# Differential attention with q and k projected feature-major, rotary rows exchanged by DMA, and attention steps split into probabilities and values

## The chip, the cores and the metric

One core of one Trainium2 chip runs the whole program. The metric is the time of one execution in microseconds, as the device measures it; the profiled execution has a span (first to last instruction) beside its time. PE is the matrix engine, DVE the vector engine, ACT the scalar engine, POOL the general engine, SP the engine that issues most of the DMA transfers. The weight loads of PE are shown as PEld; they run beside its matmuls.

## What is computed

Two layers work on 512 tokens x and 256 context tokens, 1024 wide. Each layer normalises, projects with `w_in`, and mixes three ways: differential attention (DA, 4 heads), grouped-query attention (GQ, 8 heads) and a long convolution (hyena); the three are gated and projected with `w_out`. The second layer needs its context tokens only as keys and values. The part that the change touches is DA:

```python
def _rope_1d(x, cos, sin):
    x1, x2 = jnp.split(x.astype(jnp.float32), 2, axis=-1)
    return jnp.concatenate([x1 * cos - x2 * sin, x2 * cos + x1 * sin], axis=-1)
...
def _diff_attend(q, k, v, lam):
    scale = DA_QK_DIM ** -0.5
    def body(qb):
        s = jnp.einsum('bqhcd,bkhcd->bhcqk', qb, k).astype(jnp.float32) * scale
        p = jax.nn.softmax(s, axis=-1)
        a = (p[:, :, 0] - lam * p[:, :, 1]).astype(v.dtype)
        return jnp.einsum('bhqk,bkhe->bqhe', a, v)
...
    ka_all = jnp.concatenate([ka_c, _rope_2d(ka, tab_da)], axis=1)
    oa = _rms(_diff_attend(qa, ka, va, lam), da_subln_g) * (1.0 - lam_init)
```

A head has two maps (c = 0 and 1) with 64 features each for q and k, and 128 features for v. Queries and keys of x are rotated, those of the context are not.

## The kernel before

Every fp32 product is made of three matmuls on split operands (high and low part, `mm3`, L138 to L140): high by high, high by low, low by high. There are two shapes of projection. `proj_tok` gives a pair of token tiles, tokens on partitions and features along the row: 48 matmuls of 128x256 (pst<-wh,hT). `proj_feat` gives 128 features on partitions and all tokens along the row: 24 matmuls of 128x512 for x or of 128x256 for the context (psf<-hT,wh). The token pairs are numbered 0 and 1 (x) and 2 (context).

In time a layer runs: hyena, GQ (its attention from about 280 to 560 us in layer 0, 1120 to 1360 in layer 1), DA (560 to 765 and 1330 to 1475) and `w_out` (px<-wh,yT).

DA works head by head. For each pair of x the kernel projects q and k together with `proj_tok`, rotates them in the token-major layout (DVE L1039 by the cosine, two DVE L1043 by the sine, two POOL L1046 that combine the halves), and turns the result with four PE transposes (L1050) into the same PSUM bank, features on partitions. `evac_q` copies a pair with its scale (ACT L1012) and leaves high and low parts of the two maps on opposite halves of the partitions (DVE L1015); `evac_k` makes a high tile and a low tile (ACT L1024, DVE L1027, L1028, ACT L1029, POOL memset L1023). The context's q and k come feature-major from `proj_feat` and go through the same two functions.

Attention runs in the background of the projections. A step of `da_att` is one query pair of one head: for each half of 128 queries and each map, scores S (PE L628, L629: one pair of matmuls per key pair), maximum (DVE L634), exponential (ACT L637), reciprocal; then the weighted difference of the two maps (ACT L965, DVE L966); and in the same step `pv`: transposes T of the probabilities P (PE L648), their split into ph (ACT L581) and pl (DVE L582), and the value matmuls O (PE L655 and L656 with ph, L658 with pl), followed by norm and gate. `gq_att` has the same form with a query pair of one head per step. A generator yields after each step; `att.spread(steps, units)` spreads the steps over the projections that follow, and each projection advances them. From the program's order a list scheduler with a model of the engines' times then sets the order of each engine's queue, and interleaves freely; each engine executes its own queue strictly in that order.

The buffers that set limits are: score banks S two, T one, O one, projection banks two; six P tiles, five ph/pl tiles, five tiles in the pool of the rotary temporaries, twenty tiles for q, k and v. SP issues nearly all loads and stores in order (weights raw<-in_w_in, gates gl<-gd, results yx<-tah and yx<-y, reloads yld<-yx); POOL issues the tables and yT loads.

## Time and profile before

| | us |
|---|---|
| median of 3 runs | 1595.95 (1593.34 to 1599.08) |
| profiled execution, its own time | 1593.43 |
| its span | 1591.7 |
| granted clock, mean | 0.989 |

The profile of that one execution gives, for each engine, its busy time; for windows of time the same with the granted clock of PE; and for an instruction that waits the one that released it. Matmuls overlap, so the time that one costs is read from the distance between two starts, not from its duration. The rows that matter stand below.

### The profile page before, as it was taken

What the parts mean: (1) busy time and instruction counts of PE and PEld (TensorE: products, weight loads), DVE (VectorE), ACT (ScalarE), POOL (GpSimd) and SP (SyncE); (2) the same over time, 40 slices, a digit from 0 to 9 for tenths busy, and PEclk for the clock granted to TensorE, in tenths of its full rate; (3) what the DMA queues carried; (4) which work ended last, traced back from release to release, by engine and by line L of the source; (5) the groups of instructions that cost most, each with busy time, mean ns of one, the idle gap of its engine ahead of it and who ended that gap; (6) DMA issues with size and microseconds to landing.
All of it is one profiled execution on the core that took longest, in us unless ns stands there. A gap on an engine that the chain in (4) does not pass through costs nothing.

```text
span 1591.7 us, 29098 instructions
## 1 busy us (share of the span) xinstructions
PE 1510.1 (95%) x11126; PEld 1398.6 (88%) x11126; DVE 1127.6 (71%) x2222; ACT 830.9 (52%) x1673; POOL 415.6 (26%) x451
## 2 busy tenths in 40 slices
PE   5989999999999999998999999999999999898997
PEld 3768889999898989798999977888999998898997
DVE  6789667877776475777755378869877756768755
ACT  5645243555556555566653256334546556656643
POOL 0243443212212141113002114334222222214032
PEclk9999999999999999999999999999999999999999
DMA  9437676423435253315352334674422232115441
GB/s 344 145 111 263 192 222 200 129 76 96 143 102 169 93 159 117 113 48 195 117 179 94 93 108 145 213 229 146 152 75 87 87 97 87 57 51 182 130 133 70
DMA packets 105952, 216.87 MB, mean 136 GB/s; under 512 B 11345, under 2 KB 54291, under 8 KB 105812
## 3 DMA queue, kind: packets, MB, share of 16 engines
q1 hardware_dynamic: 95300, 178.56, 34.9%
q0 software_dynamic: 9936, 35.39, 7.3%
q8 instruction: 88, 1.44, 0.4%
q10 hardware_dynamic: 576, 1.05, 0.2%
q14 instruction: 52, 0.43, 0.1%
HBM read 174.45 MB, written 40.52 MB: 135 GB/s over the span
## 4 chain that ended last, share of the span: by engine, by line
PE 79%; DVE 9%; DMA 4%; issue 3%; ACT 3%; POOL 1%; SPq 0%; POOLq 0%; DVEq 0%; ACTq 0%
PE psf L138 7%; PE psf L139 7%; PE psf L140 7%; PE pst L138 6%; PE pst L140 6%; PE pst L139 6%; PE px L138 4%; PE px L140 4%; PE px L139 4%; PE T L648 4%; PE O L658 2%; PE O L655 2%; PE O L656 2%; PE S L138 2%; PE S L140 2%
## 5 line engine op out<-in xcount | busy, mean ns | idle before, releaser
L138 PE MATMUL psf<-hT,wh 128*128 128x512 f32 (+1 forms) x768 | 267.9, 353 | 8.8 <-DVE cv L687 5.0
L138 PE MATMUL pst<-wh,hT 128*128 128x256 f32 x960 | 273.8, 285 | 0.2
L139 PE MATMUL pst<-wl,hT 128*128 128x256 f32 x960 | 273.7, 285 | 0.0
L140 PE MATMUL pst<-wh,hT 128*128 128x256 f32 x960 | 273.6, 285 | 0.0
L139 PE MATMUL psf<-hT,wh 128*128 128x512 f32 (+1 forms) x768 | 268.4, 350 | 0.0
L140 PE MATMUL psf<-hT,wl 128*128 128x512 f32 (+1 forms) x768 | 268.2, 349 | 0.0
L156 DVE TENSOR_TENSOR wl<-raw,wh 128x1024 fp32r<-128x1024 f32 x136 | 174.6, 1285 | 40.1 <-ACT wh L152 38.7
L152 ACT ACTIVATE wh<-raw 128x1024 fp32r<-128x1024 f32 x136 | 143.5, 1056 | 90.1 <-PE psf L139 34.7
L140 PEld LDWEIGHTS pst<-wh,hT 128*128 128x128 f32 x960 | 183.9, 192 | 1.7 <-issue 1.7
L138 PEld LDWEIGHTS pst<-wh,hT 128*128 128x128 f32 x960 | 184.0, 192 | 1.6 <-issue 1.1
L139 PEld LDWEIGHTS pst<-wl,hT 128*128 128x128 f32 x960 | 183.9, 192 | 0.2
L138 PE MATMUL px<-wh,yT 128*128 128x256 f32 x640 | 181.6, 284 | 1.1 <-DMA yT<-yx 0.6
L140 PE MATMUL px<-wh,yT 128*128 128x256 f32 x640 | 181.6, 284 | 0.2 <-DVE yT L1083 0.2
L139 PE MATMUL px<-wl,yT 128*128 128x256 f32 x640 | 181.5, 284 | 0.0
L637 ACT ACTIVATE P<-S,sa 128x768 f32<-128x768 f32 (+1 forms) x160 | 130.2, 814 | 87.3 <-DVE sa L634 59.1
L138 PEld LDWEIGHTS psf<-hT,wh 128*128 128x128 f32 x768 | 146.3, 191 | 29.0 <-ACT kH L1029 3.2
L140 PEld LDWEIGHTS psf<-hT,wl 128*128 128x128 f32 x768 | 146.5, 191 | 17.9 <-issue 0.8
L139 PEld LDWEIGHTS psf<-hT,wh 128*128 128x128 f32 x768 | 146.9, 191 | 17.3 <-issue 1.2
L634 DVE TENSOR_REDUCE sa<-S 128x1 f32<-128x768 f32 (+1 forms) x160 | 134.6, 841 | 21.8 <-PE S L140 11.9
L582 DVE TENSOR_TENSOR pl<-T,ph 128x512 fp32r<-128x512 f32 x156 | 107.1, 687 | 49.0 <-ACT ph L581 44.2
L581 ACT ACTIVATE ph<-T 128x512 fp32r<-128x512 f32 x156 | 92.7, 594 | 86.5 <-PE T L648 85.6
L138 PEld LDWEIGHTS px<-wh,yT 128*128 128x128 f32 x640 | 122.1, 191 | 2.1 <-ACT pm L1152 0.9
(300 smaller groups left out, 3559.8 us busy)
## 6 DMA issues: line engine op xcount, KB each, us to landing
raw<-in_w_in SPq DMA_DIRECT2D x104, 512.0 KB, 4.1
adaw<-in_ada_w SPq DMA_DIRECT2D x32, 512.0 KB, 4.4
raw<-in_w_out SPq DMA_DIRECT2D x32, 512.0 KB, 3.8
tab<-in_inv POOLq DMA_DIRECT2D x20, 512.0 KB, 4.6
tab<-in_fwd POOLq DMA_DIRECT2D x18, 512.0 KB, 5.1
adaw<-in_ada SPq DMA_DIRECT2D x16, 512.0 KB, 10.7
yT<-yx POOLq DMA_DIRECT2D x16, 512.0 KB, 7.1
gl<-gd SPq DMA_DIRECT2D x60, 128.0 KB, 2.3
```

The lines of the kernel that those rows point to most:

```text
L138: i0 = PE.matmul(ps, sh, mh, start=first, stop=False)
L139: PE.matmul(ps, sh, ml, start=False, stop=False)
L140: return i0, PE.matmul(ps, sl, mh, start=False, stop=last)
L152: ACT.activation(hi, src, AF.Copy)
L156: last_lo[0] = e.tensor_tensor(out=lo, in0=src, in1=hi.bitcast(F32), op=ALU.subtract)
L581: ACT.activation(dh, ps, AF.Copy)
L582: return DVE.tensor_tensor(out=dl, in0=ps, in1=dh.bitcast(F32), op=ALU.subtract)
L634: DVE.tensor_reduce(out=nm, in_=S[:, :n], axis=AX.X, op=ALU.max, negate=True)
L637: ACT.activation(P[:, :n], S[:, :n], AF.Exp, bias=nm, accum_out=s)
L648: PE.transpose(T[:, kk, q * 128:(q + 1) * 128], aa[q][:, (2 * i + kk) * 128:(2 * i + kk + 1) * 128], ident)
L655: PE.matmul(O, vh, ph[:, kk], start=(i == 0 and kk == 0), stop=False)
L656: PE.matmul(O, vl, ph[:, kk], start=False, stop=False)
```

## The change

First, q and k of x in DA are projected feature-major. `rope_feat(qk)` runs `proj_feat` for q (0) or k (1): ACT copies the bank to v (dv), SP issues four transfers of 32x512 (64 KB each) from v to w (dw) that swap neighbouring groups of 32 rows, DVE multiplies the bank by the cosines (L1061, df), POOL multiplies w by the sines (L1062), DVE adds the two (L1063). The tables cosD and sinD are laid out to suit, 128x512 each instead of 128x128. `evac_q` then reads halves of the sum, and `evac_k` reads all 512 columns at once into a high and a low tile per map (ACT, DVE L1049 and L1050, POOL L1047).

Second, the scores of an x query have one pair of matmuls for the 512 x keys and one pair for the 256 context keys.

Third, attention steps are skewed: `skewed` runs the probabilities of step n and then the values of step n - 1, with one more step at the end, in GQ and in DA; the gate's load moves into the values.

Fourth, the program is built with a descriptor scratch of 8192 for DMAs that software generates.

```diff
         def scores_c(c, q, kT, klist, i):
             S = pS.tile([128, 1024], F32, tag="S", name="S")
             m = slice(i * 128, (i + 1) * 128)
-            for n, kp in enumerate(klist):
-                kh, kl = kT[kp]
-                ps = S[:, n * 256:(n + 1) * 256]
-                PE.matmul(ps, q[:, c, m], kh[:, c], start=True, stop=False)
-                PE.matmul(ps, q[:, c, m], kl[:, c], start=False, stop=True)
+            for isx, lo in ([(True, 0), (False, 512)] if len(klist) > 1 else [(False, 0)]):
+                kh, kl = kT[isx]
+                ps = S[:, lo:lo + (L if isx else LC)]
+                PE.matmul(ps, q[:, c, m], kh[c], start=True, stop=False)
+                PE.matmul(ps, q[:, c, m], kl[c], start=False, stop=True)
             return S
...
+        def skewed(steps, probs, values):
+            ahead = None
+            for step in steps:
+                if step[0] != 1:
+                    slow.tick()
+                aa = probs(*step)
+                if ahead:
+                    values(*ahead)
+                ahead = (*step, aa)
+                yield
+            values(*ahead)
+            yield
...
+            yield from skewed([(j, hh) for j in qpairs for hh in range(2)], probs, values)
...
-                att.spread(2 * len(qpairs), nq + {(0, 0): -full, (0, 1): 3, (1, 0): 0, (1, 1): 1}[g, c])
+                att.spread(2 * len(qpairs) + 1, nq + {(0, 0): -full, (0, 1): 3, (1, 0): 0, (1, 1): 1}[g, c])
...
+            yield from skewed([(j,) for j in qpairs], probs, values)
...
-                def evac_k(p, ps):
-                    kh = up.tile([128, 2, 256], F32R, tag="u", name="kH")
-                    kl = up.tile([128, 2, 256], F32R, tag="u", name="kL")
+                def evac_k(isx, src):
+                    n = L if isx else LC
+                    if isx:
+                        kh, kl = [[up.tile([128, n], F32R, tag="u", name=nm) for _ in range(2)] for nm in ("kH", "kL")]
+                    else:
+                        kh, kl = [up.tile([128, 2, n], F32R, tag="u", name=nm) for nm in ("kH", "kL")]
+                        kh, kl = [[v[:, c] for c in range(2)] for v in (kh, kl)]
                     for c in range(2):
-                        POOL.memset(kl[64 - 64 * c:128 - 64 * c, c].bitcast(F32), 0.0)
...
+                        r, o = slice(64 * c, 64 * c + 64), slice(64 - 64 * c, 128 - 64 * c)
+                        POOL.memset(kl[c][o].bitcast(F32), 0.0)
+                        ACT.activation(kh[c][r], src[r], AF.Copy)
+                        DVE.tensor_tensor(out=kl[c][r], in0=src[r], in1=kh[c][r].bitcast(F32), op=ALU.subtract)
+                        DVE.tensor_copy(kh[c][o], kh[c][r].bitcast(F32))
+                    kT[isx] = (kh, kl)
...
-                for p in (0, 1):
-                    ps = proj_tok(W, p)
...
-                    DVE.tensor_tensor(out=t1.rearrange("p t c (h d) -> p t (c h) d", d=32),
-                                      in0=ps.rearrange("p t (c d) -> p t c d", d=32), in1=cb, op=ALU.mult)
...
-                    for qk in range(2):
-                        for t in range(2):
-                            PE.transpose(ps[:, qk, t * 128:(t + 1) * 128],
-                                         t1[:, t, 2 * qk:2 * qk + 2].rearrange("p c d -> p (c d)"), ident)
-                    evac_q(p, ps[:, 0])
-                    evac_k(p, ps[:, 1])
+                def rope_feat(qk):
+                    ps = proj_feat(W, qk, True)
+                    v = tp.tile([128, L], F32, tag="tp", name="dv")
+                    ACT.activation(v, ps, AF.Copy)
+                    w = tp.tile([128, L], F32, tag="tp", name="dw")
+                    for i in range(4):
+                        SP.dma_start(w[32 * i:32 * i + 32], v[32 * (i ^ 1):32 * (i ^ 1) + 32])
+                    f = tp.tile([128, L], F32, tag="tp", name="df")
+                    DVE.tensor_tensor(out=f, in0=ps, in1=cosD, op=ALU.mult)
+                    POOL.tensor_tensor(out=w, in0=w, in1=sinD, op=ALU.mult)
+                    DVE.tensor_tensor(out=f, in0=f, in1=w, op=ALU.add)
+                    return f
+
+                f = rope_feat(0)
+                for p in range(2):
+                    evac_q(p, f[:, p * 256:(p + 1) * 256])
+                evac_k(True, rope_feat(1))
                 if full:
                     evac_q(2, proj_feat(W, 0, False))
-                evac_k(2, proj_feat(W, 1, False))
+                evac_k(False, proj_feat(W, 1, False))
                 att.add(da_att(head, hh, V, qT, kT))
-                att.spread(len(qpairs), {0: nq, 1: 3 + nq - ng, 2: nq - ng, 3: 1}[head])
+                att.spread(len(qpairs) + 1, {0: nq, 1: 3 + nq - ng, 2: nq - ng, 3: 1}[head])
...
-    cosD = cp.tile([128, 4, 32], F32, tag="cosD", name="cosD")
+    cosD = cp.tile([128, L], F32, tag="cosD", name="cosD")
...
-    nc = _bacc.Bacc("TRN2", target_bir_lowering=False, num_devices=1)
+    nc = _bacc.Bacc("TRN2", target_bir_lowering=False, num_devices=1, dynamic_dma_scratch_size=8192)
```

How the queues of the engines change is shown at two places. On PE in the last DA steps of layer 1, between matmuls of `w_out`, the queue before reads, with S the scores, T the transposed probabilities, and O the values:

```order
L628 MATMUL S<-kH,qT 128x256
L629 MATMUL S<-kL,qT 128x256
L648 MATMUL T<-ident,P 128x128 x3
L655 MATMUL O<-ph,vh 128x256
L656 MATMUL O<-ph,vl 128x256
L655 MATMUL O<-ph,vh 128x256
L656 MATMUL O<-ph,vl 128x256
L658 MATMUL O<-pl,vh 128x256 x2
L648 MATMUL T<-ident,P 128x128
L628 MATMUL S<-kH,qT 128x256
```

and the queue of the changed kernel, at the place that answers to it:

```order
L628 MATMUL S<-kH,qT 128x512
L629 MATMUL S<-kL,qT 128x512
L628 MATMUL S<-kH,qT 128x256
L629 MATMUL S<-kL,qT 128x256
L648 MATMUL T<-ident,P 128x128 x4
L655 MATMUL O<-ph,vh 128x256
L656 MATMUL O<-ph,vl 128x256
L655 MATMUL O<-ph,vh 128x256
L656 MATMUL O<-ph,vl 128x256
L658 MATMUL O<-pl,vh 128x256 x2
L655 MATMUL O<-ph,vh 128x256
```

The scores of the next step now stand ahead of T, with 512 columns and 256; all four T of a key pair are followed at once by their O, and a second run of O follows directly.

On DVE at the rotary of the second DA head of layer 0 the queue before reads, with pst the projection's bank and t_8236 to t_8310 the rotary's temporaries:

```order
L1039 TENSOR_TENSOR t_8236<-pst,cosD 128x512
L1043 TENSOR_TENSOR t_8237<-pst,sinD 128x8x32 x2
L582 TENSOR_TENSOR pl<-T,ph 128x512
L1015 SCALAR_TENSOR_TENSOR qT<-pst,qT 64x256 x2
L1027 TENSOR_TENSOR kL<-pst,kH 64x256 x2
L1028 CAST kH<-kH 64x256
L1039 TENSOR_TENSOR t_8309<-pst,cosD 128x512
L1043 TENSOR_TENSOR t_8310<-pst,sinD 128x8x32 x2
```

and in the changed kernel, at the same head, with psf the bank, df the product with the cosines and dw the exchanged rows:

```order
L1061 TENSOR_TENSOR df<-psf,cosD 128x512
L582 TENSOR_TENSOR pl<-T,ph 128x512
L1063 TENSOR_TENSOR df<-df,dw 128x512
L1034 SCALAR_TENSOR_TENSOR qT<-df,qT 64x256 x4
L639 RECIPROCAL sa<-sa 128x1
L634 TENSOR_REDUCE sa<-S 128x1
L582 TENSOR_TENSOR pl<-T,ph 128x512
L1061 TENSOR_TENSOR df<-psf,cosD 128x512
L639 RECIPROCAL sa<-sa 128x1
L891 TENSOR_SCALAR P<-P,sa 128x256
L634 TENSOR_REDUCE sa<-S 128x1
L910 SCALAR_TENSOR_TENSOR y<-O,cols_250,gl 128x256
```

The multiplication L1061 and the sum L1063 of a rotary, which needs the exchanged rows, have one other operation between them for q; for k the sum comes two rows below this piece. Before, the combination was POOL's and DVE went on. On SP the eight exchanges of that head stand as one block between the stores and loads of gates and results and the loads of weights:

```order
L578 DMA gd_174<-sg 128x512
L578 DMA gd_174<-sg 128x256
L1059 DMA dw<-dv 32x512 x8
L915 DMA yx_6_125<-tah 128x256
L669 DMA gl<-gd_170 128x256
L915 DMA yx_6_125<-tal 128x256
L396 DMA adaw<-in_ada_w 128x1024 x2
L528 DMA raw<-in_w_in 128x1024 x2
```

Before, no transfer belonged to the rotary, and the rows around the block followed each other directly.

## Rows read from the trace of the kernel before

**Rows 1.** The page: busy time of each engine, share of the span, instructions.

```profile
PE 1510.1 (95%) x11126; PEld 1398.6 (88%) x11126; DVE 1127.6 (71%) x2222; ACT 830.9 (52%) x1673; POOL 415.6 (26%) x451
```

**Rows 2.** Windows: us, then busy PE, PEld, DVE, ACT, POOL; PEclk, DMA share, GB/s.

```profile
280.00:560.00 280.00, 280.00 (x2124) 260.57 (x2124) 199.64 (x438) 156.37 (x338) 59.89 (x62) 1.00 0.37 116
...
720.00:765.00 45.00, 40.36 (x306) 38.80 (x304) 34.90 (x70) 29.76 (x58) 14.38 (x25) 0.92 0.60 194
...
1370.00:1400.00 30.00, 26.50 (x201) 25.24 (x202) 20.13 (x43) 16.58 (x34) 5.29 (x9) 0.94 0.18 58
...
sum 270.00, PE 248.04 PEld 233.96 DVE 202.46 ACT 172.04 POOL 66.21; mean PE 35.43 PEld 33.42 DVE 28.92 ACT 24.58 POOL 9.46
```

**Rows 3.** Waits of PE, whole span: engine, line, releaser: us, times, longest.

```profile
PE O L655 <- ACT ph L581: 6.2, 6, 3.0
...
PE O L658 <- DVE pl L582: 3.3, 7, 1.2
...
PE S L628 <- ACT P L637: 2.9, 6, 0.6
...
PE pst L1050 <- POOL t L1046: 1.5, 1, 1.5
```

**Rows 4.** Timeline of PE, layer 0, DA's first head: start us, us, line, operation.

```profile
565.80 0.28 PE L140 MATMUL pst<-wh,hT 128*128 128x256 f32 x1
...
567.12 0.60 PE L1050 MATMUL pst<-ident,t 128*128 128x128 f32 x4
...
567.67 0.28 PE L140 MATMUL pst<-wh,hT 128*128 128x256 f32 x1
```

**Rows 5.** Timeline of PE in a stretch of feature-major projection.

```profile
229.84 0.39 PE L138 MATMUL psf<-hT,wh 128*128 128x512 f32 x1
...
231.43 0.39 PE L139 MATMUL psf<-hT,wh 128*128 128x512 f32 x1
```

**Rows 6.** Lines by form: busy, mean ns of one | idle before.

```profile
L1039 DVE TENSOR_TENSOR t<-pst,cosD 128x512 f32<-128x512 f32 x16 | 11.0, 686 | 7.4 <-PE pst L140 7.4
...
L1043 DVE TENSOR_TENSOR t<-pst,sinD 128x256 f32<-128x256 f32 x32 | 12.0, 415 | 0.0
...
L1046 POOL TENSOR_TENSOR t<-t,t 128x256 f32<-128x256 f32 x32 | 24.2, 776 | 55.0 <-DVE t L1043 41.2 <-issue 11.9 <-DVE sa L639 1.8
...
L574 ACT ACTIVATE gv<-psf 128x512 f32<-128x512 f32 x24 | 14.2, 593 | 20.5 <-PE psf L140 16.6 <-issue 3.8
...
L604 POOL TENSOR_TENSOR t<-t,t 128x512 f32<-128x512 f32 x16 | 21.6, 1350 | 59.9 <-DVE t L602 44.6 <-PE S L140 6.5 <-DVE sm L171 5.9
...
L577 DVE TENSOR_TENSOR sg<-gv,sg 128x512 f32<-128x512 f32 x24 | 17.5, 731 | 2.8 <-ACT sg L183 2.8
```

**Rows 7.** DMA issues: KB each, median us from issue to landing.

```profile
yx<-tah SPq DMA_DIRECT2D x32, 128.0 KB, 1.8
```

**Rows 8.** Timeline of SP's queue in a DA stretch.

```profile
644.75 0.38 SPq L669 DMA_DIRECT2D gl<-gd  x1
```

**Rows 9.** Timeline of PE: T groups with O directly behind them.

```profile
1370.82 0.60 PE L648 MATMUL T<-ident,P 128*128 128x128 f32 x4
...
1372.10 0.38 PE L655 MATMUL O<-ph,vv 128*128 128x256 f32 x1 [0.69 <-ACT ph L581]
...
1439.71 0.66 PE L648 MATMUL T<-ident,P 128*128 128x128 f32 x4 [0.91 <-DVE pl L582]
1440.12 0.36 PE L655 MATMUL O<-ph,vh 128*128 128x256 f32 x1
```

**Rows 10.** Windows behind the late transfer, columns as in rows 2.

```profile
753.00:757.00 4.00, 2.89 (x12) 2.08 (x12) 3.89 (x8) 2.94 (x7) 0.00 (x0) 0.72 0.62 226
757.00:761.00 4.00, 3.54 (x16) 3.54 (x17) 3.18 (x8) 2.85 (x5) 0.60 (x1) 0.50 0.00 0
```

**Rows 11.** Timeline of ACT, then PE, around the late transfer.

```profile
751.05 0.63 ACT L1082 ACTIVATE yT<-yld 128x512 fp32r<-128x512 f32 x1 [1.92 <-DMA yld<-yx]
...
753.53 0.39 PE L655 MATMUL O<-ph,vh 128*128 128x256 f32 x1 [2.96 <-ACT ph L581]
```

More of the change, by code (lines that the diff above doesn't have):

```diff
@@ L867, in layer, with probs @@
         accG = rr.tile([128, 768], F32, tag="rr", name="accG")
-        def gq_att(g, c, kT, V, qT):
-            for j in qpairs:
-                for hh in range(2):
-                    head = 4 * g + 2 * c + hh
-                    if j != 1:
-                        slow.tick()
+        def skewed(steps, probs, values):
[10 more added lines that the diff above has]
+            yield
+        def gq_att(g, c, kT, V, qT):
+            def probs(j, hh):
                     kl_ = klist_of(j)
-                    gt = gate_tile(head, j)
                     aa = []
@@ L886, in gq_att, with values @@
                         aa.append(P)
+                    return aa
+            def values(j, hh, aa):
+                    head = 4 * g + 2 * c + hh
+                    kl_ = klist_of(j)
+                    gt = gate_tile(head, j)
                     O = pv(aa, kl_, lambda kp, kk: (V[kp][0][:, kk], V[kp][1][:, kk]))
@@ L953, in da_att, with probs @@
                     yt[11, False] = (t[:, 0], t[:, 1])
-            for j in qpairs:
-                if j != 1:
-                    slow.tick()
+            def probs(j):
                 kl_ = klist_of(j)
-                gt = gate_tile(8 + head, j)
                 aa = []
@@ L968, in da_att, with values @@
                     aa.append(P0)
+                return aa
+            def values(j, aa):
+                kl_ = klist_of(j)
+                gt = gate_tile(8 + head, j)
                 O = pv(aa, kl_, lambda kp, kk: (V[kp][0][:, kk, hh * 128:(hh + 1) * 128],
@@ L989, in da_att @@
                     DVE.tensor_tensor(out=lo, in0=y, in1=h.bitcast(F32), op=ALU.subtract)
-                yield
+            yield from skewed([(j,) for j in qpairs], probs, values)
         for pr in range(2):
@@ L1008, in layer, with evac_q @@
                 qT, kT = {}, {}
-                def evac_q(p, ps):
+                def evac_q(p, src):
                     st = up.tile([128, 2, 256], F32R, tag="u", name="qT")
-                    ACT.activation(st, ps.unsqueeze(1).to_broadcast([128, 2, 256]), AF.Copy, scale=0.125)
+                    ACT.activation(st, src.unsqueeze(1).to_broadcast([128, 2, 256]), AF.Copy, scale=0.125)
                     for c in range(2):
                         r, o = slice(64 * c, 64 * c + 64), slice(64 - 64 * c, 128 - 64 * c)
-                        DVE.scalar_tensor_tensor(out=st[o, c], in0=ps[r], scalar=0.125, in1=st[r, c].bitcast(F32),
+                        DVE.scalar_tensor_tensor(out=st[o, c], in0=src[r], scalar=0.125, in1=st[r, c].bitcast(F32),
@@ L1348, in hybrid_mixer @@
         subln.append(sg)
-    cosD = cp.tile([128, 4, 32], F32, tag="cosD", name="cosD")
+    cosD = cp.tile([128, L], F32, tag="cosD", name="cosD")
     SP.dma_start(cosD, a["cosD"])
-    sinD = cp.tile([128, 4, 32], F32, tag="sinD", name="sinD")
+    sinD = cp.tile([128, L], F32, tag="sinD", name="sinD")
     SP.dma_start(sinD, a["sinD"])
@@ L1384, in _constants @@
     c["cosG"], c["sinG"] = axial(128)
-    c["cosD"], c["sinD"] = axial(64)
+    cd, sd = [v.transpose(1, 0, 2).reshape(L, 32).T for v in axial(64)]
+    c["cosD"] = np.ascontiguousarray(np.concatenate([cd] * 4))
+    c["sinD"] = np.ascontiguousarray(np.concatenate([-sd, sd] * 2))
     for n in (512, 256):
```

20 lines of the change are left out of this document (removed).

## Prediction

> **What bounds the kernel now.** I read first the busy shares. PE works 95% of the span, DVE 71%, ACT 52%, POOL 26% [rows 1]; the reader is to see that nearly every microsecond has a matmul in it, so that PE work taken away is time taken away wherever PE doesn't wait. Then the windows, stage by stage. In the GQ stage of layer 0 PE is busy 280.00 of 280 us; in the seven DA windows of both layers it is busy 248.04 of 270, so some 22 us are idle there, and the granted clock falls to 0.92 over 45 us and to 0.94 over 30 us, another 3.6 + 1.8 = 5.4 us [rows 2]. DVE is busy 202 of the same 270 (75%), ACT 172 (64%): neither is full, so what PE waits for there is a chain and not an engine's sum of work. The waits name the chain: over the whole span O waits 6.2 us for ph and 3.3 for pl (the transposed probabilities, split by ACT and DVE), and S 2.9 for P, the softmax that has to free a score bank; together 12.4 [rows 3]. The transposes of the old rotary waited once, 1.5 us.
>
> **Projections.** Matmuls are priced by the distance of their starts, as their durations overlap. From 565.80 to 567.12 eleven steps of 128x256 take 1.32 us, 0.120 each [rows 4]; from 229.84 to 231.43 seven steps of 128x512 take 1.59, 0.227 each [rows 5]. Per head and layer the change replaces 96 of the first (two token pairs of 48) by 48 of the second (q and k, 24 each): 96 x 0.120 - 48 x 0.227 = 11.52 - 10.90 = 0.62 us. Eight heads (four in each of two layers): -5.0 us. The columns streamed are the same; only the few ns that each matmul costs beside its columns go.
>
> **Transposes.** Each of 16 token pairs loses one group of four. The group starts at 567.12 and the second matmul behind it at 567.67, 0.55 us later, of which 0.12 are the one matmul between: 0.43 us a group, 16 x 0.43 = -6.9 us [rows 4].
>
> **Scores.** Each of 64 sets (8 heads x 2 query pairs x 2 halves x 2 maps) has two matmuls of 512 and two of 256 in place of six of 256: 4 x 0.120 - 2 x 0.227 = 0.026, -1.7 us. Together -13.6 us of PE work, nearly all in stages where PE works 92% of the time (248 of 270) or more. The page "TensorE: Matmul & The Clock Gate" of the Trainium skill (Back-to-back issue gap) gives a sustained 131 ns per matmul of 512 columns; by it the 384 + 128 long matmuls would save another 49 us, and the rows, at 227 ns in an undisturbed stretch [rows 5], speak against it.
>
> **Rotary.** Before: DVE 0.686 + 2 x 0.415, then POOL 2 x 0.776, then the transposes: 3.5 us from the projection's end to rows that evac_q can read [rows 4, 6]. After: ACT copies the bank (0.593, the copy of gv), SP issues four exchanges, POOL multiplies (1.350, t at L604), DVE adds (0.731, sg at L577) [rows 6]. An exchange is 64 KB; the nearest row is the 128 KB yx<-tah, 1.8 us to landing [rows 7]; an issue on SP takes 0.38 [rows 8], so the last of four starts 1.1 us behind the first. 0.6 + 1.1 + 1.8 + 1.4 + 0.7 = 5.6 us, 2.1 more than before. DVE's and ACT's work per head stays about the same and POOL's falls; what is new is a wait of DVE. L1061 (f) and L1063 (the sum) stand in its queue with one to thirteen operations between; in the q rope of the second head only one evacuation (0.7 us) is there, so DVE would stand 5.6 - 0.7 - 0.7 - 0.7 = 3.5 us with the next evacuations, reductions for softmax and weight splits queued behind L1063. PE is meanwhile in the k projection (24 x 0.227 = 5.4 us), whose weights are split already; that hides it. Without that cover PE stands the 3.5 us. Bounds for 16 ropes: -1.5 (the one old wait on POOL goes too, [rows 3]) and 16 x 3.5 = +56. I take two waits of the size of the old one, +3.0, as the first scores of a head stand far behind its projection. POOL stands waiting for the same rows; behind it are the memsets, token sums and the yT loads that w_out needs later, so its price is in the same bound. ACT's copy doesn't wait for anything but the projection, as the old copies did. On SP the exchanges are issued between weight loads and gate loads; a wait for v there delays loads that run well ahead: 0, up to the 1.9 us that the one late row of yld cost ACT [rows 11].
>
> **Skew.** A step's values now stand behind the next step's scores, so its softmax has PE work beside it. GQ has no idle time to give [rows 2]: 0. In the DA stages the ceiling is 22 + 5.4 us. The floor is no gain, as the scheduler already interleaves steps with projections. I take a third of the 12.4 us of waits named, -4.1. The step's scores also use the two score banks earlier, which can put a wait on S in place of one on O; that is why not more. The gate load moves behind the probabilities; its reader comes after all the value matmuls: 0.
>
> **Bare places.** The order of the changed kernel has ten places where a group of T is followed at once by its O, where there were four; the two pieces shown with the change are such. The trace has prices: at 1370.82 four T take until O at 1372.10, 1.28 us, of which 4 x 0.11 are their own issue: 0.84 lost; at 1439.71 the next O starts 0.41 later, nothing lost [rows 9]. Six more places: 0 to +5.0; I take the upper end, since the chain T, ACT, O is always longer than nothing. O on ph followed at once by O on pl goes from 53 places to 72; the 3.3 us of that wait [rows 3] over 53 is 0.06 each: +1.2.
>
> **Edits at nothing.** The tables cosD and sinD are 384 KB larger; three times the 1.8 us landing of 128 KB [rows 7] is 5.4 us at worst, and nothing reads them before DA's first projection at 565 us [rows 4]. The smaller scratch for descriptors concerns POOL's loads, which are issued far ahead: 0, at most a wait of the size of yld's, 1.9.
>
> **The sum**, against the profiled run of 1593.4 us (span 1591.7): 1593.4 - 5.0 - 6.9 - 1.7 + 3.0 - 4.1 + 5.0 + 1.2 = 1584.9. The median of the runs shown is 2.5 above the profiled one, so 1587.4. With bare places at nothing and two thirds of the waits gone it is 1578; with rope waits of 11 us it is 1595.
>
> **Rivals.** A, the skew does what it could: half of the ceiling goes, 13.7 us in place of 4.1, and the bare places cost nothing: 1593.4 - 13.6 - 13.7 + 3.0 + 2.5 = 1571.6; 1558 (all of the ceiling) to 1578. For it: DVE and ACT are not full. Against it: the bare places that the order shows.
>
> B, PE's saving comes back as waits: in DA, PE waits for a chain on ACT and DVE whose work doesn't shrink, so the 13.6 us turn into idle time. Then only the other terms stay: 1593.4 - 4.1 + 5.0 + 1.2 + 2.5 = 1598; with half of the 13.6 kept 1591. For it: the 22 us of idle time. Against it: in most of that stage PE is busy with projections or w_out matmuls that wait for nothing.
>
> C, slower: the exchanged rows come late, and in-order DVE holds PE. The trace has one such event: at 751.05 ACT stands 1.92 us for a DMA (yld), ph comes late, PE stands 2.96 us at 753.53 [rows 11], and the granted clock is 0.72 and 0.50 in the two windows of 4 us behind it (0.50 is the 1.2 GHz level), another 1.1 + 2.0 = 3.1 us [rows 10]: 6 us for one late transfer. It decides when PE stands more than the 11.5 us that the other terms leave (13.6 + 4.1 - 5.0 - 1.2): from two such events, or from 16 x 0.7. Half of the 16 ropes at 3 us: 1593.4 - 11.5 + 24 + 2.5 = 1608. Against it: PE has independent matmuls at 16 of 16 ropes in the program's order. The page "SBUF — State Buffer" of the Trainium skill (The DMA setup-cost knee) speaks against small transfers, with some 2 us fixed for each; paid one after another, the estimate from it is 4 x 2.15 = 8.6 us a rope, which would put this rival above the sum; no run here has such an exchange yet.
>
> D, weight loads are the limit: the kernel loses 384 + 128 + 64 = 576 of them, at 1398.6 / 11126 = 0.126 us each [rows 1] 72 us: 1593.4 - 72 + 2.5 = 1524. Against it: 512 columns take 0.227, nearly twice the 0.120 of 256, with one load each [rows 4, 5]. The page "Perfetto Trace Analysis" of the Trainium skill (Identifying the Most-Contended Engine) holds the load share to be the better measure of TensorE; if so D wins.
>
> **How the numbers follow.** About 0.3% (4.8 us) is what a measurement of this kernel can tell from no change, so "same" is 1591.2 to 1600.7. My forecast 0.50 (0.40 of it below 1591.2), A 0.13, B 0.22 (0.17 same, 0.03 faster, 0.02 slower), C 0.13 (0.11 slower), D 0.02. Faster 0.40 + 0.13 + 0.03 + 0.02 = 0.58, same 0.10 + 0.17 + 0.02 = 0.29, slower 0.13. The range runs from 1567 to 1602: it leaves out D, a little under half of A and most of C, about 0.16.
>
> **What would show it.** PE's instruction count down by 576 and its busy time in DA down with it; PE still full in the GQ stage; starts of the new projection 0.227 apart; waits of O on ph not above 10 us in total; DVE waiting on dw (L1063) with PE busy beside it. Wrong if PE's idle time in the DA windows grows by more than 10 us, with releasers that lead back to dw (C) or to ph and P (B), or if it falls below 12 (A).

## Result, and the profile after

| | us |
|---|---|
| before, median of 4 | 1596.18 (1593.34 to 1599.08) |
| changed, median of 4 | 1612.21 (1611.06 to 1617.01) |
| ratio | 1.0112 (95% interval 1.0091 to 1.0134) |
| changed, profiled execution and its span | 1611.33, 1609.5 |
| granted clock, before and changed | 0.989, 0.982 |

Slower by 1.1%, where 0.5% faster was forecast. The page's busy times of the changed kernel answer to [rows 1]:

```profile
PE 1512.3 (94%) x10550; PEld 1372.6 (85%) x10550; DVE 1133.8 (70%) x2198; ACT 834.4 (52%) x1673; POOL 411.1 (26%) x419
```

The instructions fell by 576, from 11126 to 10550, and yet PE is busy 2 us longer. Three things bear on the time. Counting the matmuls of 512, 256 and 128 columns in the two traces at their undisturbed distance (0.227, 0.120, and 0.109 for a transpose), the work is 1484.6 us before and 1471.0 after: 13.6 less, as the prediction said. PE's idle time, span less busy, goes from 81.6 to 97.2 us, +15.6. The granted clock costs at most (1 - 0.989) x 1591.7 = 17.5 us before and (1 - 0.982) x 1609.5 = 29.0 after, +11.5. Together that is +13.5 of the 17.8 us by which the span grew; the other 4.3 us this count does not resolve.

The same by layers (width; busy PE, PEld, DVE, ACT, POOL; PEclk, DMA share, GB/s), split at the last w_out matmul of layer 0. Before:

```profile
0.00:926.00 926.00, 877.35 (x6610) 805.90 (x6611) 643.43 (x1306) 475.52 (x998) 232.68 (x262) 0.99 0.46 147
926.00:1591.70 665.70, 632.72 (x4519) 592.71 (x4517) 484.21 (x917) 355.40 (x675) 182.96 (x189) 0.99 0.38 121
```

After:

```profile
0.00:939.70 939.70, 883.23 (x6321) 797.45 (x6322) 642.74 (x1294) 478.67 (x998) 231.80 (x246) 0.98 0.46 148
939.70:1609.50 669.80, 629.05 (x4231) 575.11 (x4229) 491.09 (x905) 355.75 (x675) 179.32 (x173) 0.99 0.40 123
```

PE idles 7.8 us longer in each layer. The clock differs in layer 0 alone: by the trace's clock records it stands at its lower level (1.2 GHz) for 41 us there and stood so for 17, which is up to 12 us of time. So layer 0 takes 13.7 us more and layer 1 4.1 more, though each has 6.8 us less of PE work.

The projections run as priced; the timeline of PE (start, duration) has 0.23 to 0.24 between starts in the changed kernel:

```profile
707.53 0.39 PE L139 MATMUL psf<-hT,wh 128*128 128x512 f32 x1
707.76 0.40 PE L140 MATMUL psf<-hT,wl 128*128 128x512 f32 x1
708.00 0.39 PE L138 MATMUL psf<-hT,wh 128*128 128x512 f32 x1
```

Where in the layers PE idles shows in windows by stage: in layer 0 from GQ's first scores to its last, and from there to the first w_out matmul; in layer 1 from the first w_out matmul to the end. Before:

```profile
310.00:613.00 303.00, 301.43 (x2297) 277.67 (x2296) 208.90 (x447) 167.14 (x361) 71.72 (x78) 1.00 0.39 123
613.00:763.00 150.00, 138.35 (x1086) 129.97 (x1085) 111.40 (x229) 93.71 (x192) 33.87 (x58) 0.98 0.36 113
...
1474.00:1591.00 117.00, 109.05 (x906) 108.45 (x904) 72.55 (x138) 55.33 (x123) 25.87 (x22) 0.99 0.34 107
```

After, at the places that answer to these:

```profile
312.00:625.00 313.00, 309.14 (x2266) 279.49 (x2265) 209.03 (x445) 172.96 (x365) 70.78 (x74) 0.99 0.39 120
625.00:772.00 147.00, 130.69 (x828) 113.37 (x827) 108.74 (x212) 88.50 (x181) 33.66 (x47) 0.95 0.44 137
...
1465.00:1609.00 144.00, 126.63 (x991) 120.92 (x990) 94.85 (x173) 72.36 (x156) 35.12 (x32) 0.98 0.37 120
```

DA of layer 0 idles 16.3 us where it idled 11.7, at a clock of 0.95 for 0.98. The first row's stage is 313 us long and was 303: GQ's last scores come 12 us later. Before, they stood at 613 and DA's first scores at 623; the stretch called DA ahead of the prediction, from 560 us on, begins with DA's projections, beside which GQ's attention still runs. Layer 1's last projection leaves 12 score sets of 768 columns behind it where it left 9, and w_out idles 17.4 us where it idled 8.0. PE's waits (total, times, longest) answer to [rows 3]:

```profile
PE S L628 <- ACT P L637: 7.4, 8, 2.4
PE O L655 <- ACT ph L581: 6.7, 9, 1.3
...
PE O L658 <- DVE pl L582: 4.3, 9, 0.8
PE T L648 <- DVE pl L582: 3.8, 3, 2.2
```

The last of them read before:

```profile
PE T L648 <- DVE pl L582: 1.5, 3, 0.9
```

S on P has grown from 2.9 to 7.4 us and T on pl from 1.5 to 3.8, O on ph and pl only by 0.5 and 1.0.

One event in full, at the entry into DA of layer 0. SP issues the k exchange of the first head, one transfer and, 2.2 us later, behind the stores and gate loads of GQ, the three others (0.6 us each):

```profile
583.52 0.51 SPq L1059 DMA_DIRECT2D dw<-dv  x1
...
585.69 1.79 SPq L1059 DMA_DIRECT2D dw<-dv  x3
```

DVE's timeline beside it (the brackets hold the idle time and what ended it):

```profile
587.87 0.48 DVE L910 SCALAR_TENSOR_TENSOR y<-O,cols,gl 128x256 f32<-128x256 f32 x1 [0.82 <-DMA gl<-gd]
590.89 0.69 DVE L1063 TENSOR_TENSOR df<-df,dw 128x512 f32<-128x512 f32 x1 [2.53 <-POOL dw L1062]
591.50 1.22 DVE L156 TENSOR_TENSOR wl<-raw,wh 128x1024 fp32r<-128x1024 f32 x1
592.64 0.68 DVE L407 TENSOR_TENSOR mrow<-psm,mrow 128x512 f32<-128x512 f32 x1
593.24 0.15 DVE L639 RECIPROCAL sa<-sa 128x1 f32<-128x1 f32 x1
593.31 0.94 DVE L634 TENSOR_REDUCE sa<-S 128x1 f32<-128x768 f32 x1
```

DVE stands 2.5 us for POOL and the rows, and the weight split, the modulation row (mrow) and a reciprocal queue behind L1063. PE stands some 2 to 5 us later, for mrow and for a P whose maximum is the last row above:

```profile
593.38 0.56 PE L380 MATMUL pst<-ident,mrow 98*128 98x98 f32 x4 [0.31 <-DVE mrow L407]
595.80 0.39 PE L138 MATMUL S<-kk,qh 128*128 128x256 f32 x1 [1.87 <-ACT P L637]
...
597.51 1.93 PE L405 MATMUL psm<-adaw,cs 128*32 128x512 f32 x8 [1.09 <-issue]
```

(For the third gap the profile names no releaser.) Then the clock falls. Ten-microsecond windows of the same kernel show three such places, PE at 52 to 81% busy and the clock at 0.63 to 0.86 in or just behind them; the kernel before has one in this stage, the late transfer of [rows 10]:

```profile
590.00:600.00 10.00, 6.73 (x41) 3.56 (x41) 8.96 (x18) 5.67 (x10) 3.87 (x6) 0.82 0.57 188
600.00:610.00 10.00, 10.00 (x51) 8.65 (x50) 2.37 (x7) 2.58 (x4) 0.00 (x0) 0.84 0.45 157
...
720.00:730.00 10.00, 5.17 (x19) 3.66 (x19) 8.96 (x19) 5.69 (x14) 1.46 (x2) 0.64 0.45 133
730.00:740.00 10.00, 9.49 (x45) 7.87 (x45) 5.70 (x14) 4.74 (x11) 0.61 (x2) 0.85 0.08 26
...
760.00:770.00 10.00, 7.49 (x43) 6.15 (x41) 9.93 (x16) 8.58 (x17) 4.97 (x7) 0.86 1.13 380
770.00:780.00 10.00, 8.12 (x49) 7.87 (x48) 8.96 (x21) 6.28 (x13) 0.00 (x0) 0.63 0.63 222
```

At the second and third place DVE is 90 and 99% busy in the window where PE stands. PE waits there for P, pl, ph, the norm and qT, that is for work that stands in the queues of DVE and ACT, and not directly for exchanged rows. At the second, PE's T wait for a pl that DVE makes behind the evacuation of k and two weight splits, of which the last is shown:

```profile
725.72 1.11 PE L648 MATMUL T<-ident,P 128*128 128x128 f32 x4 [2.21 <-DVE pl L582]
```

```profile
723.83 1.23 DVE L156 TENSOR_TENSOR wl<-raw,wh 128x1024 fp32r<-128x1024 f32 x1
724.98 0.68 DVE L582 TENSOR_TENSOR pl<-T,ph 128x512 fp32r<-128x512 f32 x1
```

A rotary takes longer than the 5.6 us of the sum. For the first one, ACT's copy, SP's issues, POOL's product and DVE's sum are:

```profile
571.60 0.60 ACT L1056 ACTIVATE dv<-psf 128x512 f32<-128x512 f32 x1 [1.28 <-PE psf L140]
```

```profile
572.22 2.49 SPq L1059 DMA_DIRECT2D dw<-dv  x4
```

```profile
576.28 1.30 POOL L1062 TENSOR_TENSOR dw<-dw,sinD 128x512 f32<-128x512 f32 x1 [1.39 <-DMA dw<-dv]
```

```profile
577.61 0.69 DVE L1063 TENSOR_TENSOR df<-df,dw 128x512 f32<-128x512 f32 x1 [0.55 <-POOL dw L1062]
```

From 571.6 to 578.3 that is 6.7 us; over all 16 it is 6.7 to 13.0, with a median of 7.5. The issue of a transfer between tiles takes 0.6 us on SP, not 0.38. Landing was priced well (64 KB, 2.0 us). The four transfers of an exchange overlap: from the first issue at 572.22 to POOL's product it is 4.1 us, less than half of the 8.6 that the prediction worked out for them one after another. DVE waits for these rows in 8 of 16 rotaries, 12.8 us in layer 0 and 2.2 in layer 1:

```profile
dw<-dv SPq DMA_DIRECT2D x64, 64.0 KB, 2.0
```

```profile
DVE df L1063 <- POOL dw L1062: 14.9, 8, 4.7
```

### The profile page after: what moved, and what is told of

It is laid out like the page before. It is cut to its first block, busy times and chain, and to the rows that moved or that the text cites. A ratio compares the mean times of both kernels' runs of the same rounds, so it can differ in the third digit from the quotient of the medians.

```text
span 1609.5 us, 28040 instructions
## 1 busy us (share of the span) xinstructions
PE 1512.3 (94%) x10550; PEld 1372.6 (85%) x10550; DVE 1133.8 (70%) x2198; ACT 834.4 (52%) x1673; POOL 411.1 (26%) x419
## 4 chain that ended last, share of the span: by engine, by line
PE 43%; DVE 7%; DMA 3%; ACT 3%; issue 2%; POOL 1%; SPq 0%; DVEq 0%; ACTq 0%; POOLq 0%
PE px L138 4%; PE px L140 4%; PE px L139 4%; PE psf L138 4%; PE psf L139 4%; PE psf L140 4%; PE pst L138 2%; PE pst L140 2%; PE pst L139 2%; PE T L648 2%; PE O L658 1%; DVE wl L156 1%; PE O L655 1%; PE O L656 1%; DVE sa L634 1%
## 5 line engine op out<-in xcount | busy, mean ns | idle before, releaser
L138 PE MATMUL psf<-hT,wh 128*128 128x512 f32 (+1 forms) x896 | 320.8, 362 | 7.5 <-DVE cv L687 4.5
L139 PE MATMUL psf<-hT,wh 128*128 128x512 f32 (+1 forms) x896 | 320.2, 357 | 0.0
L140 PE MATMUL psf<-hT,wl 128*128 128x512 f32 (+1 forms) x896 | 319.5, 357 | 0.0
L156 DVE TENSOR_TENSOR wl<-raw,wh 128x1024 fp32r<-128x1024 f32 x136 | 178.3, 1311 | 50.4 <-ACT wh L152 46.9
L138 PEld LDWEIGHTS psf<-hT,wh 128*128 128x128 f32 x896 | 171.3, 192 | 37.0 <-issue 5.8
L138 PE MATMUL pst<-wh,hT 128*128 128x256 f32 x704 | 200.6, 285 | 1.6 <-DVE t L602 1.2
L139 PE MATMUL pst<-wl,hT 128*128 128x256 f32 x704 | 200.8, 285 | 0.0
L140 PE MATMUL pst<-wh,hT 128*128 128x256 f32 x704 | 200.7, 285 | 0.0
L139 PEld LDWEIGHTS psf<-hT,wh 128*128 128x128 f32 x896 | 171.7, 192 | 21.9 <-issue 1.2
L140 PEld LDWEIGHTS psf<-hT,wl 128*128 128x128 f32 x896 | 171.6, 192 | 21.5
L634 DVE TENSOR_REDUCE sa<-S 128x1 f32<-128x768 f32 (+1 forms) x160 | 134.3, 840 | 17.5 <-PE S L140 8.9
L138 PEld LDWEIGHTS pst<-wh,hT 128*128 128x128 f32 x704 | 134.7, 191 | 5.7 <-issue 2.5
L139 PEld LDWEIGHTS pst<-wl,hT 128*128 128x128 f32 x704 | 134.7, 191 | 1.0 <-issue 0.8
L140 PEld LDWEIGHTS pst<-wh,hT 128*128 128x128 f32 x704 | 134.7, 191 | 0.8 <-issue 0.8
```

The source lines that it names most:

```text
L138: i0 = PE.matmul(ps, sh, mh, start=first, stop=False)
L139: PE.matmul(ps, sh, ml, start=False, stop=False)
L140: return i0, PE.matmul(ps, sl, mh, start=False, stop=last)
L156: last_lo[0] = e.tensor_tensor(out=lo, in0=src, in1=hi.bitcast(F32), op=ALU.subtract)
L634: DVE.tensor_reduce(out=nm, in_=S[:, :n], axis=AX.X, op=ALU.max, negate=True)
```

## Experiments

Theory R: the exchanged rows come late and hold the engines that stand in order behind them. Theory S: the skew makes the loss. Theory W, in later runs A: attention sets the pace of DA, so that PE work taken away there is no time. Ratios are to the kernel before, measured beside each run, with 95% intervals. A kernel's queues are ordered anew by the scheduler for each edit, and no run holds the order fixed. The later runs show that a new order may be worth some 10 us in itself (e8, e17), so a difference of that size between two kernels does not price the edit alone.

**Undoing the skew (e1), and the skew alone (e2).** In the first, `skewed` calls `values(*step, probs(*step))`; the second is the kernel before with the skew.

> The changed kernel with the skew alone undone: each attention step does its probabilities and its values together again, in GQ and DA, and the spreads are those of before. Theory R (the rotary by exchanged rows makes the loss: DVE, ACT and POOL stand in order behind the late rows, banks of the projections come free late, PE is left with attention alone): about the time of the changed kernel, 1606 to 1616 us. Theory S (the skew makes the loss): it goes below before, 1582 to 1592. Theory W (less PE work simply bares the chain of softmax): as R.

> The kernel before with the skew alone, in GQ and DA; rotary, scores and tables as before. Theory R: within 0.3% of before, 1591 to 1601 us. Theory S: slower, 1606 to 1614. Theory W: as R or a little faster, 1585 to 1596, as nothing is taken from PE's work.

Measured: 1601.38 us, 1.0036 (1.0020 to 1.0052); and 1592.52, 0.9979 (0.9959 to 0.9999). The first lies between the theories, the second where R and W have it: the skew costs the changed kernel 11 us, and by itself it gains 3, near the 4.1 of the sum. The rotary and scores without the skew are slower than before already, by 5.7 us, with the 13.6 us of PE work gone. So the two parts cost 5.7 and -3.3 apart and 17.9 together; the other 15.5 us come only with both.

**The exchange without its wait (e3), and without the skew too (e11).** The rows of `w` come from the sine table, so that q and k are not rotated.

```diff
-SP.dma_start(w[32 * i:32 * i + 32], v[32 * (i ^ 1):32 * (i ^ 1) + 32])
+SP.dma_start(w[32 * i:32 * i + 32], a["sinD"][32 * i:32 * i + 32])
```

> The changed kernel, but the four transfers of each rotary read constant rows from memory in place of the copied projection: as many transfers of the same size, which need not wait for the projection (the rotation is left out of q and k so far). Theory R with the landing as its cause: 8 to 14 of the 16 us come back, 1597 to 1604, and DVE's wait before its sum (14.9 us in the changed kernel) falls below 4. Theory S and theory W: 1608 to 1616, as the wait for the rows is then not what holds PE.

> The changed kernel with both undone that gave back 11 us each: the exchanged rows come from memory and need not wait for the projection (the rotation is left out of q and k so far), and the skew is undone. If the two losses are separate and add: 1588 to 1592 us. If they are one loss, which either removes (skewed steps that stand in DVE's queue behind late rows): 1598 to 1604.

Measured: 1601.46, 1.0042 (1.0028 to 1.0056): 11 us back, and DVE's wait before the sum falls from 14.9 to 7.8 us, not below 4. With the skew undone as well, 1607.46, 1.0076 (1.0054 to 1.0097): worse than either alone. The two don't add: with constant rows the skew gains 6 us, with exchanged rows it costs 11. The gains of single edits here can't be read as the price of what they undo.

**Other orders of the rotary.** e4 places the context's q and k between exchange and use; e14 puts k ahead of q; e15 copies the exchanged rows on with four more transfers.

> The changed kernel with the rotary cut in two in the program's order: the context's q is projected and evacuated between the exchange of x's q and its use, the context's k between the exchange of x's k and its use, so that nothing of the context stands behind the exchanged rows on DVE and ACT. Theory R with order as its cause: 5 to 12 us come back, 1600 to 1607; if only the landing's length counts and not what stands behind it, 1608 to 1614. Theories S and W: as the changed kernel, 1608 to 1616.

> The changed kernel with k (of x, then of the context) projected, rotated and evacuated ahead of q in the program's order. A head's scores wait for its last row of k, and k has the longer evacuation behind the exchange. If late keys hold attention back: the first DA scores of layer 0 come 5 to 12 us earlier and the time falls to 1600 to 1607. If not, q is now what comes late: 1609 to 1617.

> The changed kernel with twice the exchange: four transfers swap the rows into one tile, and four more copy it on, some 4.5 us more from the projection to the rotated rows in each of the 16 rotaries. If the time from projection to keys is what is paid: 6 to 16 us more, 1619 to 1629. If it is hidden beside other work, or only the order of the queues counts: 1607 to 1617.

Measured: 1618.63, 1.0142 (1.0121 to 1.0164); 1610.61, 1.0099 (1.0072 to 1.0126); 1617.11, 1.0142 (1.0117 to 1.0167). Neither order helps. With k first DA's first scores came no earlier (644.7 us for 641.1), so it is not shown whether early keys would help. Doubling the exchange costs 5 us, 0.3 for each rotary, whose chain grew from a median of 7.5 to 11.6: most of it is hidden. DVE's wait before its sum is here, in e1, e3, e14 and e15 in this order:

```profile
DVE df L1057 <- POOL dw L1056: 17.1, 9, 4.4
```

```profile
DVE df L1063 <- POOL dw L1062: 7.8, 3, 3.2
```

```profile
DVE df L1063 <- POOL dw L1062: 20.6, 9, 3.6
```

```profile
DVE df L1066 <- POOL dw L1065: 7.9, 7, 1.9
```

The times are 1601, 1601, 1611 and 1617. The wait does not go with the time: it is longest where the time is that of the changed kernel, and it halves where the time is 5 us above. So the length of DVE's wait is not the price of the rotary.

**PE work alone (e5).** The kernel before, with one of three matmuls left out in the projections of q and k (the low part of the activations):

```diff
-mm3(ps[:, i], sh, sl, Wh[:, k % 4], Wl[:, k % 4], k == 0, k == 7)
+PE.matmul(ps[:, i], sh, Wh[:, k % 4], start=k == 0, stop=False)
+PE.matmul(ps[:, i], sh, Wl[:, k % 4], start=False, stop=k == 7)
```

> The kernel before with less PE work and nothing else: the projections of DA's q and k for x leave out one of the three matmuls of each product (the low part of the activations), 8 heads x 32 x 0.120 = 30.7 us of PE, twice what the change takes away, without skew, exchange or other tables. Theory A (attention sets the pace: a layer ends a fixed stretch after DA's last head, whose scores are paced by ACT and DVE, so that PE work in front of it is no time): 1588 to 1598 us, and the stretch from the last projection to the last norm matmul grows by about what the projections shrink. Theory P (DA is bound by PE, and the change loses by its waits alone): 1562 to 1574.

Measured: 1585.54, 0.9937 (0.9916 to 0.9957). Of 30.7 us taken from PE 10 became time, a third, between the two theories and nearer to A. The page of the profiled run has, against [rows 1]:

```profile
PE 1495.9 (94%) x10870; PEld 1379.9 (87%) x10870; DVE 1125.7 (71%) x2222; ACT 830.4 (52%) x1673; POOL 416.7 (26%) x451
```

```profile
core 0: 1588.4 us, clock 0.979
```

In it PE idles 92.5 us for 81.6, and 0.021 x 1588.4 = 33.4 us go into the lower clock, against 17.5 before. But this is the slowest of the kernel's four runs (1590.25) and the one with the lowest clock. Over all four the clock is 0.979 to 0.985, in the 13 runs of the kernel before beside it 0.981 to 0.988, on the average 4 us more lost to the clock and not 16. So some 17 of the 20 us that did not become time are neither work nor clock; that they are waits of PE is likely, but the faster runs have no profile.

**A step out of the softmax chain.** ACT's scaling of the second map is folded into DVE's difference, in the kernel before (e7) and in the changed one (e8); then DVE's maximum is left out, in both (e9, e10).

```diff
-ACT.activation(P1[:, :n], P1[:, :n], AF.Copy, scale=rl)
-DVE.scalar_tensor_tensor(out=P0[:, :n], in0=P0[:, :n], scalar=r0, in1=P1[:, :n],
+DVE.scalar_tensor_tensor(out=P0[:, :n], in0=P1[:, :n], scalar=rl, in1=P0[:, :n],
                          op0=ALU.mult, op1=ALU.add)
```

> The kernel before with one step taken out of DA's softmax chain: the scaling of the second map on ACT (0.94 us per 128 queries, 33 us of ACT in all, and one hop) is folded into DVE's weighted difference, which leaves the result multiplied by the sum of the first map's exponentials; the norm that follows takes that out. PE's work is as before. Theory A: attention ends earlier, and the layers with it: 1578 to 1590 us. Theory P: 1591 to 1598.

> The changed kernel with the same step taken out of DA's softmax chain. Theory A: the gain is larger than in the kernel before, 8 to 20 us, as here attention alone sets the pace: 1592 to 1604. Theory P: the loss stands in the waits for the exchanged rows and stays: 1607 to 1614.

> The kernel before with DVE's step taken out of DA's softmax chain: the maximum of the scores (0.95 us of DVE for each of 64 score sets of 768 columns and 0.41 for the context's, some 67 us of DVE in all, and one hop of the chain) is left out, and the exponential takes a quarter of the score. PE's and ACT's work is as before. Folding ACT's step away moved nothing, so if attention has a pace, DVE sets it. Theory D (DVE's in-order queue paces DA): 1568 to 1585 us. Theory P (PE or the fixed order of the queues): 1588 to 1597.

> The changed kernel with the same step left out. Theory D: with DVE relieved the change pays what it takes from PE: at or below the kernel before without its maximum, 1560 to 1580 us, so 30 us or more under the changed kernel. If it comes down no more than the kernel before does (ratio of the two as 1.011 now), DVE's load isn't what turns the change's gain into a loss: 1590 to 1605.

Measured: e7 1594.17, 0.9984 (0.9970 to 0.9999); e8 1624.45, 1.0177 (1.0160 to 1.0194); e9 1574.64, 0.9873 (0.9849 to 0.9896); e10 1600.65, 1.0030 (1.0015 to 1.0045). ACT isn't what paces DA: its busy time falls by 31 us in e7 and the time by 2. And e8 is slower than the changed kernel by 12 us with less to do, most likely by its new order; that is not shown. Leaving out the maximum takes 58 us from DVE's busy time and 21 us from the time of the kernel before, at unchanged PE work. It also takes a step out of each chain from scores to probabilities, so whether DVE's load or the length of the chain sets the pace is not separated. The DA windows of e9, against the sum in [rows 2] (the same clock times, though layer 1 stands some 13 us earlier in e9):

```profile
sum 270.00, PE 257.14 PEld 246.75 DVE 171.07 ACT 179.15 POOL 63.87; mean PE 36.73 PEld 35.25 DVE 24.44 ACT 25.59 POOL 9.12
```

PE busy 257 of 270 for 248, DVE 171 for 202. But the changed kernel, relieved in the same way, stays 1.6% above e9 (1.1% without the relief): DVE's load in general doesn't explain the loss either.

**Which layer.** The feature-major rotary and the long scores in one layer alone, layer 1 (e13) or layer 0 (e17), the other as before, the skew in both.

> The changed kernel with the feature-major rotary and the long scores in layer 1 alone; layer 0 projects and rotates as before; the skew in both. The profiles put the loss into layer 0 (13.7 us longer, its first DA scores 18 us late) and 3.7 us into layer 1. Theory L0 (what is lost is lost at the entry into DA of layer 0, where the head's keys come late): 1589 to 1598 us, near the skew alone (1592.5). If the loss belongs to every rotary alike: 1600 to 1606.

> The mirror of the former: the feature-major rotary and the long scores in layer 0 alone, layer 1 as before, the skew in both. Theory L0: 1604 to 1613 us, nearly all of the loss. If the loss belongs to every rotary alike: 1600 to 1606.

Measured: layer 1 alone 1593.17, 0.9985 (0.9971 to 0.9999); layer 0 alone 1619.22, 1.0148 (1.0120 to 1.0177). In layer 1 the change is neither gain nor loss against the skew alone (0.9979), though it takes 6.8 us from PE. In layer 0 alone it makes all of the loss and more: e17 is 7 us above the changed kernel and 6 above the range expected. This settles which rotary and scores do the harm; the two were not tried apart. The scratch and the larger tables are in both kernels, so they are not the cause. DVE's wait for the rows (L1118 is the sum's line in these two), first with layer 1 feature-major, then with layer 0:

```profile
DVE df L1118 <- POOL dw L1117: 3.6, 3, 1.6
```

```profile
DVE df L1118 <- POOL dw L1117: 12.8, 6, 4.7
```

Eight rotaries each, 3.6 us and 12.8. And DA's first scores of layer 0, in the kernel before and in the changed one:

```profile
623.43 0.28 PE L628 MATMUL S<-kH,qT 128*128 128x256 f32 x1
```

```profile
641.07 0.40 PE L628 MATMUL S<-kH,qT 128*128 128x512 f32 x1
```

18 us late; 643.5 with the rotary in layer 0 alone, 629.6 with it in layer 1 alone, and 624 to 629 in the seven kernels here that leave layer 0's rotary as it was and were profiled beside before (e2, e5, e6, e7, e9, e12, e18). The last w_out matmul of layer 0 starts at 926.0 before, at 939.7 in the changed kernel, 940.2 with layer 0's rotary alone and 921.9 with layer 1's alone. So DA of layer 0 starts late, and the layer ends late by nearly as much. Not all of e17's loss stands in layer 0, though. Layer 1 of e17, and under it that of the skew alone (e2), have the same program and the same numbers of instructions, in another order (at 1905 of 4516 places PE's queue holds another matmul):

```profile
940.20:1619.30 679.10, 637.42 (x4519) 597.77 (x4517) 486.99 (x917) 354.99 (x675) 184.53 (x189) 0.97 0.37 118
```

```profile
919.70:1588.90 669.20, 632.83 (x4519) 592.76 (x4517) 487.19 (x917) 355.76 (x675) 181.09 (x189) 0.98 0.37 120
```

It takes 9.9 us longer, with nothing in it changed but the order of the queues, what layer 0 leaves behind, and the clock. That is how far two orders of the same work can differ, and it is more than half of the loss that is to be explained. Against its being all of it: the eleven kernels with the new rotary in layer 0 have ratios from 1.003 to 1.018 (e8 and e10, which also leave out a step of the softmax, lie above their partners e7 and e9), and the eight without it from 0.987 to 1.000.

**Tiles (e19).** The changed kernel with seven tiles in place of five for the temporaries of rotary and gates.

> The changed kernel with seven tiles in place of five in the pool that the rotary (three tiles: the copy, the exchanged rows, the product) shares with the gates' temporaries (two each). In layer 0 head 1's gates of x and of the context stand right behind head 0's rotary. If these wait for tiles that the exchange holds, and projections of PE for them: 1598 to 1606 us. If the tiles are not what is short: 1608 to 1616.

Measured: 1611.26, 1.0102 (1.0059 to 1.0145). Not the tiles.

**What they point to.** e6 is the kernel before with the skew in layer 0 alone; e12 puts the low parts of DA's weights on POOL besides; e18 joins layer 0 as before with skew and layer 1 feature-major without it.

> The kernel before with the skew in layer 0 alone. The profiles of before and of the skew alone show layer 0 6.3 us shorter and layer 1 3.5 us longer with the skew. If that is the skew's doing: 1585 to 1591 us, under the skew alone (1592.5). If it is the scatter of single profiles: 1591 to 1597.

> The kernel before with the skew in layer 0 alone (1588.6 us) and, besides, the low parts of the weights of DA's q, k and v made on POOL in place of DVE (24 of 1.2 us in both layers, 29 us of DVE; POOL is busy a quarter of the time). Theory D: 1578 to 1586 us. If DVE's load isn't the bound, or POOL delivers the weights late: 1588 to 1600.

> Each layer in the form that its profiles favour: layer 0 as before with the skew, layer 1 with the feature-major rotary and the long scores and no skew. Profiles of single kernels give layer 0 919.7 to 921.9 us with the skew (926.0 before) and layer 1 652.8 and 654.3 us feature-major without skew (656.8 before). If the two add: 1582 to 1589 us, faster than both kernels and than the skew in layer 0 alone (1588.6). If those differences are scatter: 1588 to 1595.

Measured: e6 1588.58, 0.9954 (0.9939 to 0.9969); e12 1593.99, 0.9998 (0.9982 to 1.0014); e18 1590.48, 0.9965 (0.9946 to 0.9984). e6 and e18 beat both kernels, and their intervals overlap: the feature-major layer 1 adds nothing that shows. POOL as a helper costs what it relieves: against e6 DVE's busy time falls by 8 us and not by 29, as others of its operations take longer, POOL's grows by 58, and the time by 5. So it says little of DVE's load.

## Why the prediction was wrong, point by point

- **PE work, -13.6.** Right as work (-13.6), wrong as time. The step that failed first is "PE work taken away is time taken away wherever PE doesn't wait", applied to a stage because PE is 92% busy there. e5 measures it in the kernel before: a third of what is taken from PE in DA comes back as time. By that share some 4.5 us of the 13.6 would. Rival B named this and was given 0.22; its 1598 leaves out the rotary's +3.0 and should read 1601.
- **Rotary, +3.0.** The term that was mis-sized most. With the -13.6 beside it the sum has -10.6 us, or -4.4 with the bare places; without the skew they measure +5.7 (e1). I took two waits of 1.5 us because PE has independent matmuls beside each exchange. What DVE would stand was worked out well where it was (3.5 us for q of the second head, 3.66 measured), but nothing was put down for what DVE, ACT and POOL have queued behind, which is attention. The chain took 6.7 to 13.0 us for 5.6, and the last of four issues started 1.8 us and more behind the first for 1.1. But the price is not DVE's wait as such, which e14 and e15 show to go its own way.
- **Skew, -4.1.** Right for the kernel before (-3.3, with an interval from -0.2 to -6.5). In the changed kernel it costs 11: the terms were added as if each held in the company of the others, and 15.5 of the 17.9 us come only with rotary and skew together, or with the order of the queues that both have. No term of the sum stood for this.
- **Bare places, +5.0 and +1.2.** The second was met (O on pl +1.0). The first showed as S on P (+4.5) and T on pl (+2.3) rather than as O on ph (+0.5). These are single profiles.
- **Clock.** It stood in the ceiling of rival A and in the price of one event of rival C, but not in the sum. It is 11.5 of the 17.8 us, all in layer 0; the four runs of the changed kernel have 0.978 to 0.982, the runs of the kernel before beside the experiments 0.979 to 0.991 with medians of 0.985 to 0.987.
- **Rivals.** C had the right sign and a time near the measured one (1608), with the chance 0.13. Of its events like the late transfer [rows 10, 11] three stand in the windows above where the kernel before had one, so its break-even of two more was about right. Its mechanism is shown at one of the three, at the entry into DA. D fell: 576 weight loads fewer and 26 us less PEld busy, and the time rose.
- **Signs.** That PE's idle time in DA would grow by more than 10 us, with releasers that lead back to ph and P, came true if DA's last attention beside layer 1's w_out is counted: 4.7 us in DA of layer 0, 9.4 in that w_out.
- **Range.** 1567 to 1602 ended 10 us short, as C was cut off at the top.

What is shown: the work left PE as reckoned; the new rotary and scores do harm in layer 0 under every order that was tried, and none that shows in layer 1 (e13, e18); in layer 0 DA begins late; idle time in both layers and the clock in layer 0 take all of the work saved and more. What is argued only: that layer 0 is hurt because the rotary shares its queues there with the context's q and k, the context's gates and the next layer's modulation, which layer 1 doesn't have. Undoing skew or wait gave back 11 of the 16 us each, more tiles and k ahead of q nothing that shows, and none brought the time below before. Each of these runs has a new order of the queues, and orders of the same work differ by as much. So the cause inside layer 0 stays open: which neighbour in the queue does the harm, whether it is the rotary or the long scores, and how much of it is this one order.

## What to carry to other kernels

That the busiest engine of a stage stands at 92% doesn't make its work time; here a third of it was. Before work taken from that engine is counted as time, take some away alone and look. A longer round trip between in-order engines is not priced by the cover on the engine that profits; nor, in these runs, was the time that the waiting engine stands the price. Terms that were each measured or estimated alone need not add: of the 18 us here 15 came only with two parts together. And try a change in each part of the program by itself, since here the same edit is harmless in one layer and costs 1.7% in the other.

## What the runs showed of the hardware

The clock fell at places where TensorE stood: in layer 0 of the changed kernel PE was 52 to 81% busy over 10 us at three places, and the clock granted there or just behind was 0.63 to 0.86. One profile is not enough to read the mean clock of a kernel: four runs of e5 have 0.979 to 0.985, and its profiled one is the lowest. A transfer of 64 KB between two tiles of 32 rows holds SP for 0.6 us at its issue, where a gate load takes 0.38 [rows 8]; it lands in 2.0 us, hardly other than the 1.8 of a transfer twice as large [rows 7]. Splitting a weight tile takes 2.42 us on POOL in e12, where DVE takes 1.29 (e6); with 24 of 136 splits moved, DVE's busy time fell by 8 us.
